# One step of a hybrid recurrent, convolution and MLP layer on one core: two tasks for the bonus and the values of the preparation, and landing times and dependent steps in the scheduling model

## The chip, the core and the metric

The kernel runs on one core of a Trainium2 chip. The metric is device microseconds of one execution, the median of several. The engines are TensorE (PE, matrix products and transposes), VectorE (DVE), ScalarE (ACT), GpSimd (POOL), and SyncE (SP), on whose queue all DMAs of this kernel are issued, one after the other. Tiles lie in SBUF on 128 partitions; PE writes to eight banks of PSUM, which DVE and ACT read.

## The reference

A layer with width D = 1024 for a context of 128 tokens and a latent sequence of 1024, 1152 together:

```
shift_a, scale_a, gate_a, shift_f, scale_f, gate_f = jnp.split(mod[:, None, :], 6, axis=-1)
h = _rmsnorm(x, norm1_g) * (1 + scale_a) + shift_a
z = h @ w_in
...
s_f, y_f = _wkv7_scan(s_f0.astype(f32), rh, heads(dec_f), k_fh, vh, kk, heads(a_f), reverse=False)
s_b, y_b = _wkv7_scan(s_b0.astype(f32), rh, heads(dec_b), k_bh, vh, kk, heads(a_b), reverse=True)
...
bonus = jnp.sum(rh * (k_fh + k_bh) * r_k, axis=-1, keepdims=True) * vh
g = jax.nn.sigmoid(gl) @ w_g2
o_rwkv = (yn + bonus.reshape(b, l, RWKV_WIDTH)) * g
...
mix = jnp.concatenate([o_rwkv.astype(x.dtype), o_conv.astype(x.dtype)], axis=-1) @ w_out
x = (x + gate_a * mix).astype(x.dtype)
h = _rmsnorm(x, norm2_g) * (1 + scale_f) + shift_f
f = jnp.square(jax.nn.relu(h @ w_ff1)) @ w_ff2
x = (x + gate_f * f).astype(x.dtype)
```

`mod` is `silu(c) @ w_mod + b_mod`, 6 x 1024 columns, once for the latent and once for the context vector. The change touches how `bonus` and the part `ln_b * g` that is added to it are made ready.

## The kernel before, in words

Channels lie on partitions, and the 1152 tokens are three groups of 384. Stages follow each other:

- **Startup:** loads and transposes x, makes the first 16 of 48 blocks (128 columns each) of `mod`, which the first norm needs, and `hT`, the normed input in two parts (a rounded one and its rest, so that three products with a split weight make one in full precision).
- **Preparation** (line 1154): for each of 27 column blocks of `w_in`, three groups of 24 matmuls of `hT` with the split weight `w` (`proj_task`), whose results `take_task` turns into `r_g`, `k_g`, `v_g` (three buffers each) and others. `gate_task`, `front_task` (one for each direction) and `kk_task` make the scan's operands from them and store these in DRAM. `value_task` (line 1098) goes over 4 pairs of heads and 3 groups: it adds the two directions' keys `kd_g` into the one buffer `bt_g`, multiplies by r and `r_k`, turns the values v and stores them (8 DMAs to `v_d`), sums over the head with a matmul against `ones_blk`, multiplies by v, makes the gate's product, and stores two arrays of 192 KB in `fin_d`, one from `gl_g`, one from `bt_g`. `mod_task` (line 1132) makes the other 32 blocks of `mod`: each is a DMA of 512 KB into the one buffer `wm`, 16 matmuls, a copy `R` and two small matmuls with `sel`; after the last a matrix of gates is stored in `gate_d`. `warm_task` issues filler matmuls of `ident16`.
- **Chain stage:** a new pool of buffers takes the memory of the preparation's tiles, so that its first loads (`bk`, `qr`) and POOL's fill of `Z` wait for all of that to be done with, the last stores among it. It makes the chunked scan of both directions, 36 steps of loads.
- **x1 stage** (output projection and second norm), **FFN** (first and second product), and a **tail** in which the last output tiles are summed from banks (`facc<-bank,facc`), multiplied by the gate (`late9`), added to x (`late1` and up), normed by ACT (`sf`) and scaled by DVE into the result (`facc<-facc,sf,late11`).

The order in which each engine works is fixed when the program is written, by a scheduler, `class Order` (line 28). Tasks are generators that emit operations, each with its priority. The scheduler keeps for each engine the time at which it is free, and for each tile who read and wrote it until when. `start` (line 82) says when an operation could begin: the latest end of those it depends on, plus a price `HOP` for the way from one engine to another; dependences on the same engine are left out. `run` (line 250) always issues the operation that can begin first, among those within 20 ns the one of the first task. Durations come from formulas at the helpers (`act` line 335, `tt` line 362, `stt` line 377, `dma` line 449). In this model a DMA holds its queue for bytes/350 ns (at least 480) and has landed 1900 ns later. An engine of the chip works strictly in the order so written.

## Time and profile before

| | us |
|---|---|
| median of 3 runs | 1871.28 |
| lowest and highest run | 1868.84, 1874.59 |
| the profiled execution, its own time | 1867.13 |
| its span in the trace | 1865.3 |
| PE busy in the span | 1725.0 (92%) |
| DVE busy | 1170.3 (63%) |
| ACT busy | 572.9 (31%) |

The span is the time from the first to the last instruction that the profiler recorded; the execution's own time is 1.8 us longer. In the page, the chain that ended last is followed back from the last instruction to what released each one, so it tells whose time adds up to the span. A window's busy time against its length tells whether an engine had holes there, and the list of waits says what ended these holes. A row of the timeline holds neighbouring instructions of one form; several rows may overlap, since an engine starts one while the last is still in its pipeline.

### The profile page before, as it was taken

To read this page: it belongs to the slowest core of one execution; us is meant where nothing else is said; L and a number is where in the kernel's file an instruction comes from. 1 tells how busy PE (TensorE), PEld (TensorE's weight loads), DVE (VectorE), ACT (ScalarE), POOL (GpSimd) and SP (SyncE) were. 2 spreads that over 40 slices of the span, in tenths; PEclk is the share of its full clock that TensorE was granted. 3 is DMA by queue.
4 is the path that set the end of the run, shared out by engine and by line. 5 is a ranking of instruction groups with operands and counts; after the bars stand their busy time and mean duration, and the time that the engine had idled before them with its cause. 6 is when DMAs were issued, how large, how long until landed. Compare 5 with 4: busy or idle time off the path is not lost.

```text
span 1865.3 us, 47366 instructions
## 1 busy us (share of the span) xinstructions
PE 1725.0 (92%) x20250; PEld 1535.8 (82%) x20250; DVE 1170.3 (63%) x2481; ACT 572.9 (31%) x1384; POOL 36.0 (2%) x167
## 2 busy tenths in 40 slices
PE   5899999999877878888989999999999999999996
PEld 3788888988767777777767899999999999999995
DVE  3557676777668877777655534555555555555557
ACT  5444344544244444444334421111100010000112
POOL 6000000000000000000000000000000000000000
PEclk9999999999999999999999999999999999999998
DMA  8436666665544443334144311111111111101142
GB/s 297 112 103 161 167 168 162 157 181 137 135 139 134 143 115 101 101 108 126 58 146 131 102 57 46 46 46 46 46 46 46 45 35 46 38 24 42 46 151 97
DMA packets 291449, 190.35 MB, mean 102 GB/s; under 512 B 109171, under 2 KB 274214, under 8 KB 291238
## 3 DMA queue, kind: packets, MB, share of 16 engines
q1 hardware_dynamic: 291238, 187.32, 34.5%
q8 instruction: 159, 2.61, 0.6%
q14 instruction: 52, 0.43, 0.1%
HBM read 137.44 MB, written 49.82 MB: 100 GB/s over the span
## 4 chain that ended last, share of the span: by engine, by line
PE 72%; DVE 8%; DMA 7%; issue 4%; ACT 4%; SPq 3%; DVEq 0%; ACTq 0%; POOL 0%; POOLq 0%
PE bank L440 72%; SPq L451 3%; DMA wm<-in_w_mod_dram 3%; DVE facc L362 1%; PE bank L443 1%; DMA fg<-fin_d 1%; DVE facc L377 1%; DVE x L362 1%; DVE y L362 1%; ACT mx L339 0%; ACT late L339 0%; DMA raw<-o_d 0%; ACT h L400 0%; DVE mx L362 0%; DMA late<-x_d 0%
## 5 line engine op out<-in xcount | busy, mean ns | idle before, releaser
L440 PE MATMUL bank<-hT,w 128*128 128x384 f32 (+1 forms) x2232 | 448.6, 354 | 0.0
L440 PEld LDWEIGHTS bank<-hT,w 128*128 128x128 f32 x2232 | 395.7, 191 | 26.8 <-issue 10.3
L440 PE MATMUL bank<-h,w 128*128 128x384 f32 x2304 | 409.9, 339 | 0.0
L440 PEld LDWEIGHTS bank<-h,w 128*128 128x128 f32 x2304 | 407.3, 188 | 1.2
L440 PE MATMUL bank<-w2f,f1f 128*128 128x512 f32 x1674 | 385.2, 389 | 0.0
L440 PEld LDWEIGHTS bank<-w2f,f1f 128*128 128x128 f32 x1674 | 314.0, 188 | 64.7
L362 DVE TENSOR_TENSOR facc<-bank,facc 128x512 f32<-128x512 f32 x252 | 173.9, 690 | 134.3 <-PE bank L440 133.1
L339 ACT ACTIVATE rl<-bank 128x384 f32<-128x384 f32 x96 | 47.2, 492 | 340.4 <-PE bank L440 340.4
L362 DVE TENSOR_TENSOR rl<-rl 128x384 f32<-128x384 f32 x96 | 53.4, 557 | 154.9 <-ACT rl L339 154.8
L440 PE MATMUL bank<-qr,bk 64*64 64x128 f32 x1152 | 118.6, 285 | 7.2 <-DMA bk<-kb_d 3.5
L384 ACT ACTIVATE cur<-bank 128x256 f16<-128x256 f32 (+1 forms) x286 | 98.2, 383 | 69.3 <-PE bank L440 56.1
L440 PE MATMUL bank<-cur,at 64*64 64x64 f16 x1728 | 87.0, 196 | 11.3 <-issue 6.5
L440 PEld LDWEIGHTS <-cur 64*64 64x64 f16 x2016 | 76.5, 108 | 24.3 <-issue 19.1
L440 PEld LDWEIGHTS <-at 64*64 64x64 f16 x2016 | 77.6, 108 | 19.9 <-issue 15.2
L440 PE MATMUL bank<-P,cur 64*64 64x64 f16 x1728 | 77.3, 198 | 17.4 <-issue 10.5
L362 DVE TENSOR_TENSOR P<-bank,lmask 128x256 f16<-128x256 f32 x180 | 74.8, 419 | 26.4 <-PE bank L440 22.2
L440 PEld LDWEIGHTS bank<-qr,bk 64*64 64x64 f32 x1152 | 77.6, 137 | 8.3 <-issue 7.9
L362 DVE TENSOR_TENSOR w<-raw,w 128x256 fp32r<-128x256 f32 (+3 forms) x149 | 77.1, 553 | 9.5 <-ACT w L339 7.8
L384 ACT ACTIVATE w2f<-raw 128x1024 fp32r<-128x1024 f32 x11 | 11.7, 1061 | 185.0 <-PE bank L440 184.7
L440 PE MATMUL bank<-G,bk 64*64 64x64 f32 x576 | 59.4, 226 | 3.2 <-issue 3.2
L440 PE MATMUL bank<-qr,Z 64*64 64x64 f32 x576 | 57.2, 223 | 3.4 <-issue 3.4
L440 PE MATMUL bank<-cur,P 64*64 64x64 f16 x1152 | 57.6, 198 | 2.8 <-issue 2.7
(251 smaller groups left out, 2479.9 us busy)
## 6 DMA issues: line engine op xcount, KB each, us to landing
raw<-in_w_ff_dram SPq DMA_DIRECT2D x43, 512.0 KB
wm<-in_w_mod_dram SPq DMA_DIRECT2D x32, 512.0 KB
raw<-in_w_in_dram SPq DMA_DIRECT2D x27, 512.0 KB
rf<-in_w_ff_dram SPq DMA_DIRECT2D x21, 512.0 KB
qr_d<-qr_g SPq DMA_DIRECT2D x24, 384.0 KB
kb_d<-kb_g SPq DMA_DIRECT2D x24, 384.0 KB
kt_d<-kt_g SPq DMA_DIRECT2D x192, 48.0 KB
bk<-kb_d SPq DMA_DIRECT2D x72, 128.0 KB
```

The source lines that it names most:

```text
L339: lambda e: se.activation(out=out, in_=in_, func=func, **kw),
L362: lambda e: ENG[e].tensor_tensor(out=out, in0=a, in1=b, op=op))
L377: lambda e: ve.scalar_tensor_tensor(out=out, in0=a, scalar=s, in1=b, op0=op0, op1=op1))
L384: lambda e: se.activation(out=out, in_=in_, func=AF.Copy) if e == "act"
L440: pe_op(out, lhsT, rhs, lambda e: te.matmul(out, lhsT=lhsT, rhs=rhs, start=start, stop=stop, **kw))
L443: pe_op(out, in_, identity, lambda e: te.transpose(out=out, in_=in_, identity=identity), 1)
L451: od.emit([("dma", max(480.0, n / 350.0))], [out], [in_], lambda e: sy.dma_start(out=out, in_=in_), 1900.0)
```

## The change

There are two parts. In the scheduler's model, `start` also counts a dependence on the same engine, on what wrote the operand, with 115 ns on DVE, 150 on ACT and 100 on POOL; an activation that also accumulates costs 150 ns more; and a DMA lands 1900 ns + bytes/200 after its time on the queue, which for the 512 KB of `wm` makes 6.0 us from the issue where it was 3.4. In the preparation, `value_task` is cut in two. `bonus_task` makes the product in `bt_g` and its sum over the head in a bank that it holds, one at a time; `value_task` turns and stores the values, makes the gate's product, multiplies the held bank by v into v's own buffer, frees the bank, and stores the second array from there, so that `v_g` is free only with that store's issue. The number of operations that these tasks make is unchanged.

```diff
--- before.py
+++ after.py
@@ -38,6 +38,9 @@
     HOP = {("pe", "dve"): 205.0, ("pe", "act"): 205.0, ("dve", "pe"): 145.0, ("act", "pe"): 175.0,
            ("act", "dve"): 150.0, ("dve", "act"): 130.0, ("act", "pool"): 170.0, ("pool", "dve"): 80.0,
            ("dve", "pool"): 150.0, ("pool", "act"): 110.0, ("pool", "pe"): 150.0}
+
+
+    SAME = {"dve": 115.0, "act": 150.0, "pool": 100.0}
     SLACK = 20.0
     GLUE = -1.0
     LOAD = 1290.0
@@ -88,8 +91,12 @@
         for wr, bs in ((False, bi), (True, bo)):
             for nm, p0, p1, f0, f1 in bs:
                 for q0, q1, g0, g1, te_, en, w in self.log.get(nm, ()):
-                    if (wr or w or nm in self.banks) and p0 < q1 and q0 < p1 and f0 < g1 and g0 < f1 and en != eng:
-                        t = max(t, te_ + self.HOP.get((en, eng), 70.0))
+                    if p0 < q1 and q0 < p1 and f0 < g1 and g0 < f1:
+                        if en != eng:
+                            if wr or w or nm in self.banks:
+                                t = max(t, te_ + self.HOP.get((en, eng), 70.0))
+                        elif w and en in self.SAME:
+                            t = max(t, te_ + self.SAME[en])
         return t
 
     def emit(self, opts, outs, ins, fn, tail=0.0, pe=None, table=None):
@@ -334,7 +341,7 @@
 
     def act(out, in_, func=AF.Copy, **kw):
         x = aps(kw.get("scale"), kw.get("bias"))
-        d = (52 if in_psum(in_) else 94) + 47 * len(x) + size(in_) / 1.2
+        d = (52 if in_psum(in_) else 94) + 47 * len(x) + size(in_) / 1.2 + (150 if "accum_out" in kw else 0)
         od.emit([("act", d)], [out] + aps(kw.get("accum_out")), [in_] + x,
                 lambda e: se.activation(out=out, in_=in_, func=func, **kw),
                 table=TABLES.get(func))
@@ -448,7 +455,8 @@
 
     def dma(out, in_):
         n = size(out) * 4 * out.ap[0][1]
-        od.emit([("dma", max(480.0, n / 350.0))], [out], [in_], lambda e: sy.dma_start(out=out, in_=in_), 1900.0)
+        od.emit([("dma", max(480.0, n / 350.0))], [out], [in_], lambda e: sy.dma_start(out=out, in_=in_),
+                1900.0 + n / 200.0)
 
     def split(src, hi, lo, eng="dve"):
 
@@ -1095,37 +1103,48 @@
                     turned(kt_d[j, d, :, cs].rearrange("p c a k -> p (c a) k"), t)
                     flag(kt_g.append, t)
 
+        bonus = []
+
+        def bonus_task():
+
+            t = bt_g[0]
+            for j in range(4):
+                for g in range(NN):
+                    q = 3 * j + g
+                    yield lambda: (j, g, 0) in kd_done and (j, g, 1) in kd_done
+                    tt(t, kd_g[0], kd_g[1], ALU.add)
+                    mark(done, ("kd", q))
+                    yield lambda: ("r", j, g) in got
+                    stt(t, r_g[q % 3], par("rk", j), t, ALU.mult, ALU.mult)
+                    use(q, "r")
+                    yield lambda: ("v", j, g) in got and len(bonus) == 0
+                    ps = ps_get([128, NW])
+                    bank = hold(ps)
+                    mm(ps, ones_blk, t)
+                    flag(bonus.append, (ps, bank))
+
         def value_task():
             for j in range(4):
                 for g in range(NN):
                     gs = slice(g * NW, (g + 1) * NW)
                     q = 3 * j + g
-                    yield lambda: (j, g, 0) in kd_done and (j, g, 1) in kd_done
-
-                    t = bt_g[0]
-                    tt(t, kd_g[0], kd_g[1], ALU.add)
-                    mark(done, ("kd", q))
-                    yield lambda: ("r", j, g) in got
-                    stt(t, r_g[q % 3], par("rk", j), t, ALU.mult, ALU.mult)
-                    use(q, "r")
 
 
                     yield lambda: ("v", j, g) in got
                     v, vt = v_g[q % 3], vt_g[0]
                     blocks_t(vt.rearrange("p c h k -> p (c h k)"), v)
                     turned(v_d[j, :, 6 * g:6 * g + 6, :], vt)
-                    ps = ps_get([128, NW])
-                    mm(ps, ones_blk, t)
-                    tt(t, ps, v, ALU.mult)
-                    use(q, "v")
-                    yield lambda: ("sg", g) in got
+                    yield lambda: ("sg", g) in got and len(bonus) > 0
+                    pb, bank = bonus.pop(0)
                     ps = ps_get([128, NW])
                     mm(ps, lw_g[:, 128 * j:128 * j + 128], sg_s[:, gs])
+                    tt(v, pb, v, ALU.mult)
+                    free(bank)
                     mul(gl_g[0], ps, par("lnw", j))
-                    stt(t, t, par("lnb", j), ps, ALU.add, ALU.mult)
+                    stt(v, v, par("lnb", j), ps, ALU.add, ALU.mult)
                     dma(fin_d[j, 0, :, gs], gl_g[0])
-                    dma(fin_d[j, 1, :, gs], t)
-
+                    dma(fin_d[j, 1, :, gs], v)
+                    use(q, "v")
 
         PACE1 = 8000.0
 
@@ -1152,7 +1171,7 @@
 
         numbered = list(enumerate(blocks))
         od.run([(0, part(sp, lambda: False)), (1, gate_task(), 4), (1, front_task(0), 0), (1, front_task(1), 0), (0, kk_task()),
-                (2, value_task(), 2), (3, proj_task(numbered), 2), (1, take_task(81), 0), (2, mod_task(), 2),
+                (2, bonus_task(), 2), (2, value_task(), 2), (3, proj_task(numbered), 2), (1, take_task(81), 0), (2, mod_task(), 2),
                 (9, warm_task(lambda: nproj[0] >= 2))])
 
         fs.close()
```

As the model sets the order of all stages, the order changes in many places. Three follow. The names are tiles with their buffer's number, and the line numbers of the changed kernel are 7 higher.

PE in the middle of the preparation, a stretch with blocks of `mod` (`wm`, 16 matmuls, of which the order shows eight in a row) among projection matmuls (`hT`); before:

```order
L440 MATMUL bank0_94<-wm_800,sc_105 32x128 x8
L440 MATMUL bank2_96<-hT_73,w2_1_69 128x384 x3
L440 MATMUL bank1_95<-sel_107,R1_801 128x2
L440 MATMUL bank2_96<-hT_73,w2_1_69 128x384 x2
L440 MATMUL bank0_94<-hT_73,w2_0_68 128x384 x14
L440 MATMUL bank5_99<-wm_800,sc_105 32x128 x8
L440 MATMUL bank0_94<-hT_73,w2_0_68 128x384 x3
L440 MATMUL bank1_95<-kk_j0_831,ones_blk_120 128x384
L440 MATMUL bank2_96<-sel_107,R1_801 128x2
L440 MATMUL bank0_94<-hT_73,w2_0_68 128x384 x7
L440 MATMUL bank2_96<-hT_73,w2_0_68 128x384 x7
L440 MATMUL bank5_99<-wm_800,sc_105 32x128 x8
```

and now:

```order
L447 MATMUL bank0_94<-wm_780,sc_105 32x128 x8
L447 MATMUL bank1_95<-hT_73,w2_1_69 128x384 x3
L447 MATMUL bank5_99<-sel_107,R1_781 128x2
L447 MATMUL bank1_95<-hT_73,w2_1_69 128x384 x4
L447 MATMUL bank0_94<-hT_73,w2_0_68 128x384 x19
L447 MATMUL bank5_99<-kk_j0_811,ones_blk_120 128x384
L447 MATMUL bank0_94<-hT_73,w2_0_68 128x384 x5
L447 MATMUL bank4_98<-wm_780,sc_105 32x128 x8
```

Between the uses of `wm` stood 19 and 17 matmuls of `hT`, and now 31 stand between two.

SP's queue at the end of the preparation, from a group's `fin_d` on (`v_d` are the values, `o_d` the convolution's result, `bk0` the chain stage's first load); before:

```order
L451 DMA fin_d_81<-gl_g0_833 128x384
L451 DMA fin_d_81<-bt_g0_832 128x384
L451 DMA gate_d_88<-R1_801 32x128
L451 DMA v_d_85<-vt_g0_829 32x6x32 x8
L451 DMA fin_d_81<-gl_g0_833 128x384
L451 DMA fin_d_81<-bt_g0_832 128x384
L451 DMA bk0_4736<-kb_d_83 128x256
```

and now:

```order
L458 DMA wm_780<-in_w_mod_dram 128x8x128
L458 DMA fin_d_81<-gl_g0_813 128x384
L458 DMA fin_d_81<-v_g1_807 128x384
L458 DMA v_d_85<-vt_g0_809 32x6x32 x4
L458 DMA o_d_86<-oc0_831 128x384
L458 DMA v_d_85<-vt_g0_809 32x6x32 x4
L458 DMA wm_780<-in_w_mod_dram 128x8x128
L458 DMA fin_d_81<-gl_g0_813 128x384
L458 DMA fin_d_81<-v_g2_808 128x384
L458 DMA gate_d_88<-R1_781 32x128
L458 DMA bk0_4715<-kb_d_83 128x256
```

The loads of the last two blocks of `mod` (`wm`) now stand among the last stores, and `gate_d` behind the last `fin_d`.

DVE in the tail, one output tile after the other; before:

```order
L362 TENSOR_TENSOR facc_17188<-bank2_96,facc_17188 128x512
L377 SCALAR_TENSOR_TENSOR facc_17188<-facc_17188,sf_17187,late11_21766 128x1024
L362 TENSOR_TENSOR facc_17188<-bank0_94,facc_17188 128x512
L362 TENSOR_TENSOR facc_17188<-facc_17188,late9_21764 128x1024
L362 TENSOR_TENSOR facc_17188<-facc_17188,late2_21757 128x1024
L362 TENSOR_TENSOR facc_17188<-bank5_99,facc_17188 128x512
L377 SCALAR_TENSOR_TENSOR facc_17188<-facc_17188,sf_17187,late11_21766 128x1024
```

and now:

```order
L369 TENSOR_TENSOR facc_17167<-bank7_101,facc_17167 128x512
L369 TENSOR_TENSOR facc_17167<-facc_17167,late1_21735 128x1024
L369 TENSOR_TENSOR facc_17167<-bank6_100,facc_17167 128x512
L369 TENSOR_TENSOR facc_17167<-facc_17167,late9_21743 128x1024
L384 SCALAR_TENSOR_TENSOR facc_17167<-facc_17167,sf_17166,late11_21745 128x1024
L369 TENSOR_TENSOR facc_17167<-bank3_97,facc_17167 128x512
L369 TENSOR_TENSOR facc_17167<-facc_17167,late2_21736 128x1024
L369 TENSOR_TENSOR facc_17167<-bank1_95,facc_17167 128x512
L369 TENSOR_TENSOR facc_17167<-facc_17167,late9_21743 128x1024
L384 SCALAR_TENSOR_TENSOR facc_17167<-facc_17167,sf_17166,late11_21745 128x1024
```

Before, the scaling (`sf`) comes behind one bank sum of the next tile; now it comes behind that and the product of the next tile with `late9`.

## Rows read from the trace of the kernel before

**Rows 1.** The page, part 4: the chain of work that ended last, its share of the span by engine.
```profile
PE 72%; DVE 8%; DMA 7%; issue 4%; ACT 4%; SPq 3%; DVEq 0%; ACTq 0%; POOL 0%; POOLq 0%
```

**Rows 2.** The windows by stage, core 0: start and end, us, busy us (x instructions) of PE, PE's weight loads, DVE, ACT and POOL, then granted clock of PE, DMA share and GB/s. In order: startup, preparation up to the end of the last projection matmul, the end of the preparation, chain stage, x1 stage, FFN, tail.
```profile
0.00:66.00 66.00, 41.79 (x392) 27.94 (x392) 32.83 (x82) 40.91 (x77) 32.22 (x135) 0.94 0.84 264
66.00:505.20 439.20, 423.68 (x2669) 381.76 (x2670) 303.98 (x665) 187.01 (x414) 2.61 (x24) 0.98 0.56 147
505.20:522.30 17.10, 7.63 (x15) 3.63 (x13) 5.03 (x10) 5.94 (x10) 0.24 (x2) 0.78 0.46 128
522.30:945.00 422.70, 355.51 (x12697) 313.38 (x12698) 324.11 (x959) 187.02 (x578) 0.91 (x6) 0.98 0.39 112
945.00:1057.00 112.00, 103.85 (x488) 84.89 (x488) 64.36 (x101) 46.76 (x119) 0.00 (x0) 0.98 0.44 143
1057.00:1801.00 744.00, 744.00 (x3781) 684.41 (x3780) 393.51 (x614) 90.08 (x149) 0.00 (x0) 1.00 0.14 43
1801.00:1865.30 64.30, 48.54 (x215) 39.83 (x213) 46.48 (x51) 15.20 (x39) 0.00 (x0) 0.90 0.44 172
```

**Rows 3.** The timeline of PE at the start of the preparation: start us, busy us, engine, line, operation, out<-in and shapes, count, and in brackets the idle time before it and what ended it.
```profile
66.07 0.59 PE L440 MATMUL bank<-sel,R 128*128 128x2 f32 x2 [3.35 <-ACT R L384]
```

**Rows 4.** The chain of work in the preparation, two of its pieces, loads of `wm`: start us, us from issue to landing.
```profile
230.11 3.81 DMA wm<-in_w_mod_dram
...
430.02 5.86 DMA wm<-in_w_mod_dram
```

**Rows 5.** The waits of PE from 66 to 505.2: engine, tile and line, what it waited for, us in total, times, longest us.
```profile
PE bank L440 <- DMA wm<-in_w_mod_dram: 14.3, 16, 2.8
PE bank L440 <- ACT R L384: 3.4, 1, 3.4
PE bank L440 <- ACT kk_j L339: 0.8, 1, 0.8
```

**Rows 6.** The timeline of PE in the preparation: the first row of a block of `w_mod` after a wait, twice, and a long run of projection matmuls in between.
```profile
180.05 0.88 PE L440 MATMUL bank<-wm,sc 128*32 128x128 f32 x16 [2.42 <-DMA wm<-in_w_mod_dram]
...
441.80 19.49 PE L440 MATMUL bank<-hT,w 128*128 128x384 f32 x111
...
484.71 1.08 PE L440 MATMUL bank<-wm,sc 128*32 128x128 f32 x16 [2.81 <-DMA wm<-in_w_mod_dram]
```

**Rows 7.** Windows in the preparation, columns as in rows 2 (the granted clock is the number after the five engines).
```profile
180.00:190.00 10.00, 9.95 (x71) 9.32 (x75) 5.79 (x13) 4.31 (x9) 0.11 (x1) 0.83 0.72 179
370.00:390.00 20.00, 17.73 (x116) 16.26 (x115) 10.38 (x23) 8.55 (x21) 0.22 (x2) 0.91 0.67 175
480.00:500.00 20.00, 17.18 (x96) 16.45 (x96) 14.59 (x31) 3.04 (x8) 0.00 (x0) 0.83 0.49 140
```

**Rows 8.** The timeline of DVE at the start of the chain stage: two operations of which the second reads what the first wrote, and a row of two that don't depend on each other.
```profile
524.35 0.69 DVE L362 TENSOR_TENSOR G<-bank,wmask 128x512 f32<-128x512 f32 x1 [7.59 <-PE bank L440]
525.07 0.29 DVE L362 TENSOR_TENSOR at<-G,eye 128x128 f16<-128x128 f32 x1
...
533.28 0.76 DVE L362 TENSOR_TENSOR P<-bank,lmask 128x256 f16<-128x256 f32 x2 [0.51 <-ACT cur L384]
```

**Rows 9.** The chain of work at the end of the preparation: start us, us, what.
```profile
509.06 2.09 DMA fin_d<-bt_g
...
511.24 0.57 DVE bt_g L362
...
517.35 1.95 DMA fin_d<-bt_g
```

**Rows 10.** The timeline of SP's queue there: start us, us on the queue, engine, line, what, count.
```profile
512.97 3.70 SPq L451 DMA_DIRECT2D v_d<-vt_g  x8
...
519.42 0.32 SPq L451 DMA_DIRECT2D bk<-kb_d  x1
```

**Rows 11.** The waits of PE in the chain stage, 522.3 to 945.
```profile
PE bank L440 <- issue: 42.1, 55, 1.8
PE bank L440 <- DVE P L362: 5.5, 14, 1.6
...
PE bank L440 <- DVE Al L377: 2.3, 2, 1.3
```

**Rows 12.** The waits of PE in the x1 stage, 945 to 1057.
```profile
PE bank L443 <- DVE mx L371: 4.4, 7, 1.3
```

**Rows 13.** The timeline of DVE in the tail: one output tile in the middle, and the last two bank reads.
```profile
1812.12 1.28 DVE L377 SCALAR_TENSOR_TENSOR facc<-facc,sf,late 128x1024 f32<-128x1024 f32 x1 [1.18 <-ACT sf L339]
...
1814.04 2.48 DVE L362 TENSOR_TENSOR facc<-facc,late 128x1024 f32<-128x1024 f32 x2
...
1818.30 1.28 DVE L377 SCALAR_TENSOR_TENSOR facc<-facc,sf,late 128x1024 f32<-128x1024 f32 x1 [1.18 <-ACT sf L339]
...
1856.81 0.68 DVE L362 TENSOR_TENSOR facc<-bank,facc 128x512 f32<-128x512 f32 x1
1857.53 1.42 DVE L362 TENSOR_TENSOR facc<-facc,late 128x512 f32<-128x512 f32 x2
```

**Rows 14.** The timeline of PE in the tail: the last of a bank's matmuls in the middle, and the last of all.
```profile
1816.06 0.84 PE L440 MATMUL bank<-w,f1f 128*128 128x512 f32 x3
...
1848.70 0.84 PE L440 MATMUL bank<-w,f1f 128*128 128x512 f32 x3
```

**Rows 15.** The page, part 6: the DMA issues of one form, count and size of each.
```profile
bk<-kb_d SPq DMA_DIRECT2D x72, 128.0 KB
```

## The prediction

> **What bounds the kernel now.** I read the chain of work first, then the windows by stage, then the waits and the timeline of each stage in which the engine named there stood still. The chain is TensorE (PE) for 72% of the span, and transfers are 7% of it [rows 1]. So the time is PE's work plus the stretches in which PE stands still, and a stage is worth looking at only where PE has holes. By stage PE's busy time and holes are [rows 2]: startup 41.8 of 66.0 us; preparation 423.7 of 439.2; its end, a gap of 17.1 us in which the last projection is done and the chain stage has no data, 7.6 busy; chain stage 355.5 of 422.7; x1 stage 103.9 of 112.0; FFN 744.0 of 744.0; tail 48.5 of 64.3.
>
> The profiled execution took 1867.13 us for a span of 1865.3; the median of the three runs shown is 1871.28, 4.15 above it. I sum against the profiled execution and add 4.15 at the end. A measurement of this kernel can tell about 0.3% (5.6 us) from no change.
>
> **The change, part by part.** No engine gets or loses more than a handful of operations: twelve multiplications change their operands, one bank is held longer, some 20 filler matmuls go. What changes is the order.
>
> *Startup.* PE's long hole at its end is 3.35 us for an `R` copy [rows 3], which stands on ACT behind three pairs of an h and an hT copy, each of which waits for VectorE (DVE). In the new order it stands behind one pair less. A third of the hole is 1.1; bounds are the whole hole (−3.4) and, if the second weight load comes later behind the loads of `wm`, +1. I take −1.
>
> *Preparation: when the 32 blocks of `w_mod` land.* All share one buffer: a block's 16 matmuls wait for its load, and the next load for them. The model had a landing 3.4 us after the issue (1.5 of queue, 1.9 of tail), the rows have 3.81 to 5.86 [rows 4]. Since the scheduler believed the shorter figure, it put block matmuls too early, and PE, which is in order, stood there with the projection matmuls queued behind: 14.3 us in 16 waits, at most 2.8 [rows 5]. Between such uses stood 17 to 20 projection matmuls in the worst places, and one takes 0.176 us (19.49/111, [rows 6]): 3.0 to 3.5 us of cover for loads of 3.8 and more. The changed model has 6.0 us (1.5+1.9+2.6). Of the 31 distances between two blocks 9 were at most 20 matmuls; in the new order it is one of the first 29, and most are 26 to 160, 4.6 us and more. I take −12 of the 14.3. The bounds are −14.3, and −5 if SP issues the loads late, since it works in order and a load also stands behind stores whose data come late.
> The same figure bears the Trainium skill's rule on the price of a transfer ("DMA: Bandwidth & Descriptors", section "Anatomy of one DMA — SWDGE (gpsimd) path": about 2.0 us fixed plus the bytes over 436 GB/s, for another issue path than this one). For 512 KB that is an estimate of 3.2 us, close to the old model, by which the old distances would hardly stall and this term would be about −3. The loads in the rows are 0.6 to 2.7 us longer, so here the trace decides.
>
> *The clock behind the waits.* The granted clock fell in three places: its mean was 0.83 in the 10 us from 180, 0.91 in the 20 from 370 and 0.83 in the 20 from 480 [rows 7], mixtures of the full 2.4 and of 1.2 GHz, and 1.7, 1.8 and 3.4 us are lost there, together 6.9. The holes of 2.42 us up to 180.05 and of 2.81 up to 484.71 [rows 6] lie right before or in them. If the holes go, these go: −5, bounds −6.9 and 0.
>
> *The last two blocks.* In the new order their matmuls stand behind the last projection matmul: 2 x 0.64 to 0.88 us [rows 6] leave the stretch, −1.5 with their copies' small holes, and go to the end of the preparation, below.
>
> *New waits.* `value_task` now waits for a bank that `bonus_task` fills, and the bonus matmul waits for DVE's product. PE has the projections to put there. Same-engine steps get 115 to 150 ns more in the model, and rows show a dependent operation only 0.03 us behind its predecessor's end (524.35+0.69 to 525.07, [rows 8]), so the new model is wrong there by some 0.1 us, in the direction that leaves slack. I put +3.5 for stalls that the order creates elsewhere (0 to +8; the waits of PE in this stretch other than for `wm` sum to 4.2 now, [rows 5]). Preparation: −12−5−1.5+3.5 = **−15**, from −24 to 0.
>
> *The end of the preparation.* Before, the last group's bonus was late because `bt_g` was released only when its store had landed, 2.09 us after its issue: the last sum is at 511.24, the last store is issued at 517.35 and lands 1.95 later [rows 9], and the first load of the chain stage is issued at 519.42 [rows 10], 14.2 us after the last projection matmul (505.2, the border in [rows 2]). POOL's fill of `Z` waits for the same store. Now `bt_g` comes free at its matmul, and the last bonus is done under the projections; that chain is gone. But something else is late: the load of the last `w_mod` block stands on SP behind the store of a group's results, eight stores of values and one of `o_d`, and it waits for the block before, whose 16 matmuls stand behind the last projection. By the rows: eleven issues of 3.70/8 = 0.46 us [rows 10], the first when the values are ready, about 0.9 before that matmul's end (an estimate), so the issue is at +4.1, the landing at +8.2 (4.1, nearer to the short end of [rows 4]), 16 matmuls at half the clock to +9.4, copy, selection, the gate's transpose and copy (five steps of about 0.5) to +12, the store of `gate_d`, its landing of 2 us [rows 9] at +14.1. First load at +14.1 against +14.2: **0**, bounds −2 and +3.
>
> *Chain stage.* Nothing is edited, but the order of DVE changes: pairs in which an operation reads what the one just before it wrote fall from 58 to 23. Two independent ones of 0.42 us took 0.76 together, so the second started 0.08 before the first's end; the dependent one starts 0.03 after [rows 8]: 0.11 x 35 = 3.9 us of DVE's time. PE's waits for DVE in the stage are 5.5 (`P`) and 2.3 us (`Al`); its largest is 42.1 of unnamed "issue" [rows 11], which this doesn't touch. I take −3. Since a new order of 12,700 matmuls may fall either way, the bounds are −8 (all of these waits) and +10.
> The Trainium skill's "VectorE: DVE Perf Modes", section "The DRAIN you can't avoid", has the next operation held until the pipe is empty, semaphore or not, so that reordering earns nothing. The 0.34 us between the starts of two operations of 0.42 us disagrees. This is rival B.
>
> *x1 stage.* Such pairs 74 to 46; PE waits 4.4 us for `mx` of DVE [rows 12]. 28 x 0.11 = 3.1 at most, mostly off the path: −1 (−3 to +2).
>
> *FFN.* Pairs 210 to 140, but PE is busy 744.0 of 744.0 at clock 1.00 and DVE for 393.5 [rows 2]: 0. If that cover fails, 70 x 0.11 = 7.7 us.
>
> *Tail.* This I can count. Before, DVE's period for one output tile is 6.18 us (1812.12 to 1818.30), of which it idles 1.18 for ACT's `sf` (the last scaling stands right behind the tile's own sum and has to wait for square, sum and root); PE's is 5.44, two banks of (1848.70−1816.06)/12 = 2.72 [rows 13, 14]. So DVE is the bound: PE ends at 1849.54, and the last read of a bank is at 1856.81. In the new order the next tile's bank sum (0.68) and first product (2.48/2 = 1.24) stand between, 1.92 us, more than the 1.78 that ACT now takes from the end of the tile's own sum (1814.04+2.48 = 1816.52) to its scaling at 1818.30. DVE's work per tile is then 6.18−1.18 = 5.0 us, under PE's 5.44, so PE sets the pace and DVE has no backlog: last bank read at about 1849.6+0.3, then sum, products and sum of the last tile 0.70+0.72+1.25+0.72+0.72 to 1854.0, where before it was 1858.95 (1857.53+1.42). **−5** (−5.5 to −3.5: one tile may still wait).
>
> Sum: −1−15+0−3−1+0−5 = **−25**. 1867.13−25 = 1842.1; with 4.15 for the median, 1846.
>
> **The rivals.** A: the waits of the preparation *move*. The blocks come no later than PE asks because SP is in order, behind stores of 0.4 us each, and what is not lost in the preparation comes at its end, when the last blocks hold the first loads. For it: in the new order the last two blocks do stand behind the last projection. Against: the early distances did grow. Preparation −3 instead of −15, end +4: 1846+12+4 = 1862.
> B: the DVE reordering earns nothing (chain and x1 stage 0): 1846+4 = 1850.
> C: the chain stage gains more, since PE's 42.1 us of "issue" are really short waits for DVE and ACT that the trace names nothing for, and a third of them goes: 1846−12 = 1834.
> D, slower: the chain stage is 36 steps (72 loads of `bk`, two directions [rows 15]), 11.7 us each, and DVE is busy 324 of its 423 us. If a too careful model puts an operation on the chain's way ahead of the next link in each step, this costs its length: one `G` product of 0.69 us [rows 8] is 36 x 0.69 = 25, 1849+25 = 1874, no change; a `G` and a `P` product (0.69+0.42) are 40, 1889. It ends slower above 0.77 us a step ((25+5.6−3)/36). Against: the model's new term is small and DVE has 99 us free.
>
> **How the numbers follow.** Forecast 1846: 0.48. A 0.17, B 0.12, C 0.10, D with one product 0.08, with two 0.05. The range 1834 to 1862 takes in C's and A's times and the bounds of the unknown terms nearest to the forecast (chain stage −8 to +10). Faster by over 0.3% (below 1865.7): forecast, A, B, C, 0.87, less 0.02 for an A that gets worse: 0.85. Within 0.3%: 0.08+0.02 = 0.10. Slower (above 1876.9): 0.05.
>
> **What would show it.** PE's waits for `wm` fall from 14.3 to about 2, and no window of the preparation shows a clock under 0.95; first `bk` load 14 us behind the last projection matmul, with `gate_d` and no longer `fin_d` ahead of it; the chain stage within 10 us of 423; in the tail the wait for `sf` on DVE falls from 8.8 us to under 2, and the last bank read follows PE's end by about 5 us. Wrong would be: waits for `wm` that stay above 8 us, a first load later than 17 us behind the last projection, or a chain stage beyond 433 us.

## The result, and the profile after

| | before | after |
|---|---|---|
| median, us | 1871.72 (4 runs) | 1819.38 (4 runs) |
| lowest and highest | 1868.84, 1874.59 | 1815.72, 1826.61 |
| the profiled execution, its own time | 1867.13 | 1815.72 |
| its span | 1865.3 | 1814.0 |

The ratio is 0.9725, interval 0.969 to 0.9761: 2.75% faster, against 1846 and 1834 to 1862 forecast. The gain is twice the forecast one and lies outside the range.

To compare stages I cut both traces at the same events: end of the last projection matmul, then the starts of the first matmul of the chain stage (`qr,bk`), of its last (`G,bk`), of the first of the FFN (`h,w`) and of the last of all, and the end. The windows after (columns as in [rows 2]), without the startup:

```profile
60.70:481.10 420.40, 415.90 (x2648) 373.55 (x2648) 310.26 (x683) 175.91 (x399) 3.61 (x24) 1.00 0.59 155
481.10:497.60 16.50, 7.25 (x48) 4.19 (x48) 2.77 (x8) 6.40 (x13) 0.24 (x2) 0.69 0.48 137
497.60:899.10 401.50, 343.11 (x12625) 306.09 (x12625) 313.85 (x942) 181.59 (x574) 0.91 (x6) 0.98 0.40 115
899.10:1003.20 104.10, 102.58 (x520) 83.49 (x515) 63.68 (x105) 49.41 (x124) 0.00 (x0) 1.00 0.46 148
1003.20:1803.30 800.10, 800.10 (x4040) 731.88 (x4039) 428.91 (x647) 113.33 (x203) 0.00 (x0) 1.00 0.17 54
1803.30:1814.00 10.70, 0.43 (x2) 0.01 (x1) 5.71 (x8) 3.54 (x10) 0.00 (x0) 0.65 0.26 108
```

and before at these events, where [rows 2] has other borders:

```profile
61.50:505.20 443.70, 424.89 (x2688) 382.46 (x2689) 306.42 (x670) 190.17 (x421) 2.61 (x24) 0.98 0.56 146
...
522.30:930.70 408.40, 343.20 (x12621) 304.55 (x12621) 317.01 (x945) 183.04 (x570) 0.91 (x6) 0.98 0.40 113
930.70:1048.80 118.10, 108.12 (x516) 86.06 (x517) 67.66 (x110) 47.58 (x119) 0.00 (x0) 0.97 0.40 131
...
1849.20:1865.30 16.10, 0.34 (x2) 0.00 (x0) 10.95 (x13) 3.59 (x11) 0.00 (x0) 0.61 0.24 98
```

| us | before | after | difference | forecast |
|---|---|---|---|---|
| startup and preparation | 505.2 | 481.1 | −24.1 | −16 |
| end of the preparation | 17.1 | 16.5 | −0.6 | 0 |
| chain stage | 408.4 | 401.5 | −6.9 | −3 |
| x1 stage | 118.1 | 104.1 | −14.0 | −1 |
| FFN | 800.4 | 800.1 | −0.3 | 0 |
| behind the last matmul | 16.1 | 10.7 | −5.4 | −5 |
| span | 1865.3 | 1814.0 | −51.3 | −25 |

The x1 stage alone holds half of what the forecast lacks. Not only PE's idle time fell there (10.0 to 1.5 us) but its busy time too (108.12 to 102.58). The granted clock was 0.97 and is 1.00, which is 3.5 us of 118.1. Of the other 2 us about half is work that left the stage: from one cut to the next the traces have 260 matmuls of `hT` by `w` of 0.227 us before, and 255 after.

PE's waits in the preparation after, where [rows 5] had 14.3 us for `wm` and 3.4 for `R`:

```profile
PE bank L447 <- ACT kk_j L346: 3.6, 4, 1.9
PE bank L447 <- DMA wm<-in_w_mod_dram: 1.6, 2, 0.9
```

PE's waits in the x1 stage, before and then after:

```profile
PE bank L443 <- DVE mx L371: 4.2, 6, 1.3
PE bank L443 <- ACT h L400: 3.7, 1, 3.7
PE bank L440 <- DVE y L362: 2.0, 1, 2.0
```

```profile
PE bank L450 <- DVE mx L378: 0.9, 2, 0.5
PE bank L447 <- ACT f L346: 0.6, 1, 0.6
```

Of 9.9 us 1.5 are left. Where the two large ones came from, ACT's timeline before shows (the row behind the dots is a copy of a loaded block of `o_d`, on which the `h` rows follow):

```profile
958.74 1.06 ACT L339 ACTIVATE mx<-x 128x1024 f32<-128x1024 f32 x1 [2.72 <-issue]
959.70 0.18 ACT L339 ACTIVATION_READ_ACCUMULATOR mx<-x 128x1 f32 x1
959.92 0.29 ACT L339 ACTIVATE ss<-ss,eps 128x1 f32<-128x1 f32 x1
960.25 0.20 ACT L339 ACTIVATE ss<-ss 128x1 f32<-128x1 f32 x1
...
969.62 0.31 ACT L384 ACTIVATE hT<-raw 128x128 fp32r<-128x128 f32 x1 [4.78 <-DMA raw<-o_d]
969.84 5.69 ACT L400 ACTIVATE h<-bank,modc,s 128x128 f32<-128x128 f32 x16
```

```profile
960.48 0.75 DVE L371 TENSOR_SCALAR mx<-x,ss 128x1024 f32<-128x1024 f32 x1 [0.17 <-ACT ss L339]
```

```profile
971.38 0.66 PE L443 MATMUL bank<-ident,mx 128*128 128x128 f32 x4 [3.65 <-ACT h L400]
```

First, the statistics: from the start of the square (958.74) to the start of the scaling into `mx` on DVE (960.48) are 1.74 us. By the formulas of the old model this is 947 (square) + 142 + 95 (the two small activations) + 150 (to DVE) = 1.33 us; by the new one, with 150 for the accumulator and 150 behind each, 1.78. So PE's transposes of `mx` were planned 0.4 us too early by this, and PE waited for `mx` six times. Second, the copy of a loaded block waited 4.78 us for its DMA on ACT, which is in order, with the 16 `h` rows behind it, for which PE stood 3.65 us. Both are the same fault as with `wm`: the model believed a thing ready that was not. But for this load of 64 KB the new price is no truer to speak of: 2.4 us from the issue in the old model, 2.7 in the new one, and 4.6 in the trace (issued at 964.93, landed at 969.54).

The tail on DVE after, where [rows 13] had 1.18 us idle ahead of each scaling and the last bank read 7.3 us behind PE's end:

```profile
1800.20 1.28 DVE L384 SCALAR_TENSOR_TENSOR facc<-facc,sf,late 128x1024 f32<-128x1024 f32 x1
...
1803.77 0.69 DVE L369 TENSOR_TENSOR facc<-bank,facc 128x512 f32<-128x512 f32 x1
1804.38 0.68 DVE L369 TENSOR_TENSOR facc<-facc,late 128x512 f32<-128x512 f32 x1
...
1809.15 1.28 DVE L384 SCALAR_TENSOR_TENSOR facc<-facc,sf,late 128x1024 f32<-128x1024 f32 x1 [0.60 <-ACT sf L346]
```

Of DVE's waits for `sf` in the tail, 8.8 us before by the prediction, this is left:

```profile
DVE facc L384 <- ACT sf L346: 1.8, 2, 1.2
```

The last bank read starts at 1803.77, just at PE's end, 1803.73 (last row below):

```profile
1802.89 0.84 PE L447 MATMUL bank<-w,f1f 128*128 128x512 f32 x3
```

The end of the preparation after, SP's queue and PE:

```profile
483.29 1.91 SPq L458 DMA_DIRECT2D v_d<-vt_g  x4
485.30 0.40 SPq L458 DMA_DIRECT2D wm<-in_w_mod_dram  x1
...
486.41 0.38 SPq L458 DMA_DIRECT2D fin_d<-v_g  x1
493.01 0.33 SPq L458 DMA_DIRECT2D gate_d<-R  x1
494.53 0.33 SPq L458 DMA_DIRECT2D bk<-kb_d  x1
```

```profile
489.64 1.08 PE L447 MATMUL bank<-wm,sc 128*32 128x128 f32 x16 [5.75 <-DMA wm<-in_w_mod_dram]
491.17 0.59 PE L447 MATMUL bank<-sel,R 128*128 128x2 f32 x2 [0.45 <-ACT R L391]
```

The load of the last block of `w_mod` stands behind the stores, PE waits 5.75 us for it, `gate_d` follows at 493.01 and the first `bk` load at 494.53, 13.4 us behind the last projection matmul.

### The profile page after: what moved, and what is told of

It is laid out like the page before. It is cut to its first block, busy times and chain, and to the rows that moved or that the text cites. A ratio compares the mean times of both kernels' runs of the same rounds, so it can differ in the third digit from the quotient of the medians.

```text
span 1814.0 us, 47292 instructions
## 1 busy us (share of the span) xinstructions
PE 1709.2 (94%) x20229; PEld 1527.7 (84%) x20229; DVE 1156.1 (64%) x2470; ACT 568.8 (31%) x1395; POOL 37.7 (2%) x167
## 4 chain that ended last, share of the span: by engine, by line
PE 80%; DVE 6%; issue 4%; DMA 4%; SPq 3%; ACT 2%; DVEq 0%; POOL 0%; ACTq 0%; POOLq 0%
PE bank L447 79%; SPq L458 3%; DMA wm<-in_w_mod_dram 2%; PE bank L450 1%; DMA zs<-in_state_rwkv_fwd_dram 0%; ACT cur L391 0%; DVE w L369 0%; DMA raw<-o_d 0%; DMA kt_d<-kt_g 0%; DVE facc L369 0%; ACT kk_j L346 0%; DVE kt_g L454 0%; DVE kb_g L369 0%; DMA xt<-in_x_sample_dram 0%; ACT h L407 0%
## 5 line engine op out<-in xcount | busy, mean ns | idle before, releaser
L447 PE MATMUL bank<-hT,w 128*128 128x384 f32 (+1 forms) x2232 | 439.9, 349 | 0.0
L447 PEld LDWEIGHTS bank<-hT,w 128*128 128x128 f32 x2232 | 388.1, 188 | 25.6 <-issue 9.8
L447 PEld LDWEIGHTS bank<-h,w 128*128 128x128 f32 x2304 | 407.3, 188 | 1.2
L447 PE MATMUL bank<-qr,bk 64*64 64x128 f32 x1152 | 115.9, 286 | 5.1 <-issue 2.9
L447 PEld LDWEIGHTS <-cur 64*64 64x64 f16 x2016 | 75.3, 108 | 21.1 <-issue 15.9
L447 PE MATMUL bank<-cur,at 64*64 64x64 f16 x1728 | 83.0, 196 | 7.9 <-issue 5.4
L369 DVE TENSOR_TENSOR w<-raw,w 128x256 fp32r<-128x256 f32 (+3 forms) x149 | 78.0, 553 | 17.5 <-ACT w L346 13.3
L391 ACT ACTIVATE w2f<-raw 128x1024 fp32r<-128x1024 f32 x10 | 10.6, 1061 | 184.7 <-PE bank L447 184.7
```

The source lines that it names most:

```text
L369: lambda e: ENG[e].tensor_tensor(out=out, in0=a, in1=b, op=op))
L391: lambda e: se.activation(out=out, in_=in_, func=AF.Copy) if e == "act"
L447: pe_op(out, lhsT, rhs, lambda e: te.matmul(out, lhsT=lhsT, rhs=rhs, start=start, stop=stop, **kw))
```

## The experiments

All stage lengths below are cut at the same events; "wm" is PE's wait for `wm` from 60 us up to the last projection matmul (in e2 and n1 one wait of 5.1 and one of 5.0 us of it end at 63 us, ahead of the preparation). The chain stage before is cut 0.2 us earlier here than above, at its last matmul's start. Each ratio is against runs of the kernel before on the same chip; the stages come from one profile each, and the chips differ: one for e1 to e4, others for n1 to n3 and m0, for e5, s1, a0 and k0, and for e6, e7, a1 and m1.

| run | ratio (95%) | last projection | gap | chain | x1 | tail | wm |
|---|---|---|---|---|---|---|---|
| before | | 505.2 | 17.1 | 408.2 | 118.3 | 16.1 | 14.3 |
| after | 0.9725 (0.969 to 0.9761) | 481.1 | 16.5 | 401.5 | 104.1 | 10.7 | 1.6 |
| e1_landing | 0.9901 (0.9883 to 0.9919) | 474.3 | 42.4 | 407.3 | 109.4 | 16.5 | 0.3 |
| e2_steps | 0.9866 (0.9846 to 0.9886) | 490.9 | 22.7 | 402.8 | 110.1 | 10.7 | 17.5 |
| e3_two_tasks | 0.9924 (0.9902 to 0.9946) | 501.1 | 10.8 | 403.4 | 116.9 | 16.2 | 9.3 |
| n1_no_landing | 0.9839 (0.9812 to 0.9865) | 494.4 | 13.8 | 397.8 | 108.1 | 10.7 | 15.9 |
| n2_no_steps | 0.9928 (0.9906 to 0.995) | 478.0 | 41.9 | 395.9 | 106.2 | 16.2 | 2.2 |
| n3_no_split | 0.9788 (0.9768 to 0.9807) | 471.7 | 32.5 | 397.2 | 103.5 | 10.6 | 0 |
| e4_steps_late | 0.9936 (0.9916 to 0.9957) | 503.7 | 18.6 | 409.0 | 111.6 | 10.6 | 13.4 |
| e5_landing_late | 0.9987 (0.9972 to 1.0001) | 503.0 | 18.0 | 411.2 | 116.5 | 16.3 | 13.1 |
| e6_act_steps_late | 0.9943 (0.9923 to 0.9964) | 507.1 | 17.1 | 403.3 | 110.9 | 10.8 | 13.9 |
| e7_dve_steps_late | 0.995 (0.9929 to 0.997) | 505.9 | 16.8 | 401.0 | 115.3 | 12.3 | 14.3 |
| s1_other_order | 0.9975 (0.9958 to 0.9991) | 502.0 | 19.1 | 408.6 | 115.9 | 16.1 | 14.6 |
| a0_after_again | 0.9717 (0.969 to 0.9743) | 481.2 | 17.2 | 398.1 | 104.0 | 10.7 | 0.9 |
| k0_one_task_blocks_first | 0.9738 (0.9712 to 0.9765) | 483.6 | 18.8 | 403.0 | 104.8 | 10.6 | 2.0 |
| m0_blocks_first | 0.9708 (0.9689 to 0.9728) | 477.6 | 13.2 | 397.5 | 104.8 | 10.6 | 0 |
| a1_after_beside | 0.97 (0.9655 to 0.9745) | 479.2 | 16.3 | 394.9 | 103.8 | 10.7 | 0.2 |
| m1_blocks_first_beside | 0.9675 (0.9633 to 0.9717) | 477.4 | 13.4 | 390.0 | 104.8 | 10.6 | 0 |

**One part alone** (e1 to e3). The edits are the three parts of the diff above, each put into the kernel before by itself.

e1: 

> The kernel before with one line changed: a DMA lands 1900 ns + bytes/200 after its queue time in the model. Theory (each part of the change acts where its model was wrong): the waits of PE for wm fall from 14.3 to under 4 us and the last projection matmul ends near 486 instead of 505.2; x1 stage (last matmul of the chain to the first of the FFN) stays at 118 +- 4 us, tail behind the last matmul at 15.8; about 1852. Rival (any new order falls another way, whatever the model says): the preparation gains under 8 us, or the x1 stage moves by more than 8.

e2: 

> The kernel before with the dependent steps alone (same-engine prices and 150 ns for an accumulating activation). Theory: x1 stage 118.2 to about 105, tail behind the last matmul 15.8 to 10.5, chain stage 408 to about 403, preparation within 4 us of 505.2 with the waits for wm still above 10; about 1848. Rival (any new order): the x1 stage moves by less than 5 us or the preparation by more than 10.

e3: 

> The kernel before with bonus and values as two tasks, the model untouched. Theory: the waits for wm stay (over 10 us), the gap between the last projection matmul and the chain stage's first matmul falls from 17.1 to 11 to 15 us, x1 stage and tail unchanged; 1866 to 1873. Rival (the two tasks carry the preparation's gain): the last projection matmul ends 10 us or more earlier, 1860 or less.

e1 behaves as the theory says in the preparation, and far beyond: the last projection ends 31 us earlier, the wait for `wm` is gone, and the gap behind it grows from 17 to 42 us, which the theory did not have. Its chain of work there (start us, us, what):

```profile
488.56 3.90 DMA wm<-in_w_mod_dram
492.51 1.12 PE bank L440 x16
493.65 3.88 DMA wm<-in_w_mod_dram
497.57 1.13 PE bank L440 x16
...
```

Five blocks of `w_mod` now stand behind the last projection, one load and 16 matmuls after the other, 5.05 us each, since all share one buffer. This is the mechanism of my rival A, at full size, and landing times alone do it. The x1 stage moved by 9 us where the theory had 4 at most; that is the rival's sign (more than 8), and e5 takes it up. e2: the tail as expected, the x1 stage at 110 where I had 105; but the preparation gained 14 us with the wait for `wm` at 17.5, so the theory missed there, and the rival's sign (more than 10) came in; the last section has the reason. e3: the gap fell to 10.8 and the waits for `wm` to 9.3, both under what I gave, and the total to 0.9924, below it too; 5 us of it stand in the chain stage. In its order the last block stands 359 projection matmuls ahead of the end, and what is left is the last group's stores.

**One part left out** (n1 to n3).

n1: 

> The changed kernel with the old landing time (1900 ns): steps and two tasks alone. Theory (the landing time takes the preparation's waits away and by itself also pushes the last blocks of w_mod behind the projections): waits for wm above 10 us again, last projection matmul 490 to 496 instead of 481.1, but the last block is 365 projection matmuls early, so the gap to the chain stage is 9 to 13 us instead of 16.5; tail 10.6; about 1826. Rival (the landing time does nothing of the gain once the steps are right): 1819 or less.

n2: 

> The changed kernel without the dependent steps: landing time and two tasks. Theory (steps carry the tail and part of the x1 stage; without them the blocks of w_mod are late again, six of them stand behind the last projection matmul): tail 16, x1 stage 108 to 114, gap to the chain stage 40 to 55; 1848 to 1862. Rival (the two tasks carry the end of the preparation, not the steps): gap under 20, 1830.

n3: 

> The changed kernel with bonus and values in one task as before: landing and steps. Theory (the split only shortens the end of the preparation): last projection matmul 478 to 486, gap 20 to 27 instead of 16.5, x1 stage 102 to 108, tail 10.6; 1822 to 1832. Rival (the split is needed for most of the gain): above 1840.

Totals were written against 1871.7, and on this chip the kernel before took 1859.53; measured were 1826.63 (n1), 1845.66 (n2) and 1817.73 (n3). By stages n1 and n2 came as the theory has it, but for a gap of n1 0.8 us longer (13.8) and an x1 stage of n2 2 us shorter; n1's total is 0.9839 where 1826 of 1871.7 is 0.976, so the landing time is worth more beside the other two than I gave. n3's tail and x1 stage came too; its preparation is shorter (471.7) and its gap longer (32.5) than I gave. Seen at the chain stage's first matmul (last projection plus gap) the parts add up: from 522.3 landing takes 5.6 us, steps 8.7 and the two tasks 10.4, 24.7 in sum, and all three together take 24.7 (497.6). That is a coincidence: left out of the three, landing is worth 10.6 us there (n1, 508.2), steps 22.3 (n2, 519.9) and the two tasks 6.6 (n3, 504.2), 39.5 in sum. What the landing time gains before the last projection (31) it gives back in the gap (25); beside it the steps shorten the gap by 25 us (n2's 41.9 to 16.5) and the two tasks by 16 (n3's 32.5), while the steps alone lengthen it (e2, 22.7). In totals, 1.0, 1.3 and 0.8% alone make 3.1, against 2.75 to 3.0 for all, which tells as little.

**From the x1 stage on only** (e4 to e7). Everything up to there keeps the order of before; the model is switched at the call that plans the x1 stage (the last hunk of e4's edit, without its other lines).

```diff
+        od.SAME = {"dve": 115.0, "act": 150.0, "pool": 100.0}
         od.run([(0, part(ot, lambda: False), 0), (0, part(o3t, lambda: False), 0), (1, x1_task(0)), (1, x1_task(1))] +
```

e4: 

> The kernel before with the dependent steps counted only from the x1 stage on (x1, FFN, tail); everything up to there is in the order of before. Theory (the statistics' steps on ACT were believed too short, so that PE's transposes stood too early): nothing moves up to 930 us, x1 stage 118.2 to 104 to 110, tail 15.8 to 10.5; about 1855. Rival (the x1 stage's gain came from what it took over from the chain stage, or by luck): x1 stage 115 to 121, only the tail gains, 1866.

e5 (the landing time in place of the steps): 

> The kernel before with the new landing time only from the x1 stage on; everything up to there is in the order of before. Theory (ACT's copy of a loaded o_d block stood in the queue ahead of the h rows for which PE's transposes waited 3.65 us; a truer landing puts it behind): no wait of PE for ACT h over 1.5 us, x1 stage 118.3 to 108 to 114, tail unchanged at 16; about 0.996 of before. Rival (e1's shorter x1 stage was carried over from the chain stage): x1 stage 116 to 121, ratio 0.999 to 1.001.

e6 (of the steps ACT's alone): 

> The kernel before with ACT's steps alone (150 ns after its own writer, 150 ns for an accumulating activation) from the x1 stage on. Theory (the row of small activations between a tile's sum and its scaling was believed too short): tail 10.6, waits for mx under 2.5 us, x1 stage 111 to 115; 0.993 to 0.996. Rival (DVE's steps carry it): tail 15 to 16, waits for mx above 3.5.

e7 (DVE's alone): 

> The kernel before with DVE's steps alone (115 ns after its own writer) from the x1 stage on. Theory (ACT's steps carry it): the scaling still stands ahead of the next product in the tail, 14 to 16 us, waits for mx 3 to 5 us, x1 stage 115 to 119; 0.998 to 1.000. Rival: tail 10.6, x1 stage 112 or less.

PE's waits in the x1 stage of e4 and of e5:

```profile
PE bank L445 <- DVE y L367: 1.7, 1, 1.7
PE bank L448 <- ACT h L405: 1.6, 1, 1.6
PE bank L448 <- DVE mx L376: 1.4, 4, 0.6
```

```profile
PE bank L444 <- DVE mx L372: 6.4, 7, 1.5
PE bank L441 <- DVE y L363: 1.9, 1, 1.9
```

Against 4.2 (`mx`), 3.7 (`h`) and 2.0 (`y`) before: the steps take `mx` to 1.4 and halve `h`; the landing time takes `h` away, as the theory has it, but `mx` rises to 6.4, so that the stage gains 2 us (116.5, as the rival has it) and the total nothing that can be told. So a hole removed by one price is given back at the place where the model is still wrong. That both together from the x1 stage on would make the 14 us is not shown, since no run has just that. Nor are steps needed for most of it: with landing and two tasks planned throughout, and no steps, n2 has 106.2 us and a clock of 1.00 in the stage, and e1, with landing alone, 109.4. Part of that is work that stands ahead of the stage there (248 matmuls of `hT` by `w` in it for 260, about 2.7 us); why the landing time gains the rest from the start on (n2 12 us, e1 9) and only 2 from the x1 stage on stays open. e4's total is 0.9936, where I had 1855 of 1871.7, 0.991, and its x1 stage 2 us longer than I gave. e6 carries the tail and as much of the x1 stage as e4, as expected; e7's tail (12.3), its wait for `mx` (2.2) and its total lie below what I gave, so DVE's steps do part of it too.

**Another order without a truer model** (s1: slack of 40 ns for 20).

```diff
-    SLACK = 20.0
+    SLACK = 40.0
```

> The kernel before with the scheduler's slack at 40 ns instead of 20: another order with no truer model in it. Theory (orders as such don't gain): total within 0.7% of before, x1 stage 113 to 122, tail 15.5 to 16.5, waits for wm above 8 us; single stages may move 5 us either way. Rival (before was an unlucky order and any other gains 1% or more): ratio 0.99 or less.

Every stage and wait stays within about 3 us of before, total −0.25%, as the theory has it. That a new order as such brings 1% or more is refuted for this one other order.

**The blocks of `w_mod` first** (m0, k0, a0, a1, m1).

```diff
-                (2, bonus_task(), 2), (2, value_task(), 2), (3, proj_task(numbered), 2), (1, take_task(81), 0), (2, mod_task(), 2),
+                (2, bonus_task(), 2), (2, value_task(), 2), (3, proj_task(numbered), 2), (1, take_task(81), 0), (1, mod_task(), 2),
```

m0: 

> The changed kernel with the priority of the task that makes the blocks of w_mod at 1 instead of 2: the last block then stands 504 projection matmuls ahead of the end instead of behind it, and 22 or more stand between any two. Theory (of the 16.5 us at the end of the preparation some 7 are the last blocks): gap 8 to 11, waits for wm under 4 us, the rest as in the changed kernel; about 1812. Rival (the gap is held by the last stores of values anyway): gap 15 to 17, 1819.

k0: 

> Landing and steps with bonus and values in one task, and the blocks of w_mod at priority 1. Theory (what the one task costs at the end is mostly the blocks that it leaves behind the projections): last projection matmul 470 to 477, gap 15 to 20 (the store of bt_g before the last bonus stays), ratio 0.967 to 0.973, within 4 us of m0_blocks_first. Rival (the split is needed): gap over 25, ratio 0.976 or more.

a0: 

> The changed kernel once more, beside the others of this call. Both theories: ratio to before 0.969 to 0.976; stages as in its first profile (481.1, gap 16.5, chain 401.5, x1 104.1, tail 10.7) within 3 us.

a1: 

> The changed kernel, on the chip of the next run. Both theories: ratio 0.969 to 0.976, gap 16 to 17.5.

m1: 

> The changed kernel with the blocks of w_mod at priority 1, on the chip of the run before. Theory (the last blocks hold the first loads, and the rest is as before): 5 to 10 us under the changed kernel, of them 3 at the gap. Rival (the two are the same and the first comparison was one of two chips): within 3 us.

With the blocks first the gap is 13.2 and 13.4 against 16.3 to 17.2: 3 us of it were the last blocks, not the 7 that I expected (m0's 8 to 11 us; its rival had 15 to 17), because eight stores of values and the last `fin_d` then end last:

```profile
481.40 3.74 SPq L458 DMA_DIRECT2D v_d<-vt_g  x8
485.23 0.39 SPq L458 DMA_DIRECT2D fin_d<-gl_g  x1
485.72 0.38 SPq L458 DMA_DIRECT2D fin_d<-v_g  x1
487.80 0.32 SPq L458 DMA_DIRECT2D bk<-kb_d  x1
```

The chain stage's first matmul comes at 490.8 in both, against 495.5 to 498.4 in the three profiles of the changed kernel. On one chip (a1, m1) the medians are 1807.18 and 1803.74, with runs that overlap: about 0.2%, between my 5 to 10 us and the rival's 3, which these runs don't settle. k0's gap is 14 us shorter than n3's, but its last projection comes 12 us later, against my 470 to 477: in the preparation PE is busy 5.6 us longer (415.5 for 409.9), with three blocks that n3 has behind the last projection, and idle 4.7 us longer. Its gap of 18.8 refutes the rival's 25; its ratio of 0.9738 lies between theory and rival, and the interval (0.9712 to 0.9765) holds both 0.973 and 0.976. On the same chip the changed kernel has 1813.89 us and k0 1817.79, 0.2%, so what the split is worth with the blocks first is small and not settled.

## Why the prediction came out too small

*Right, with size:* the waits for `wm`: 14.3 to 1.6, −12.7 where I took −12; new waits +2.8 (`kk_j` 0.8 to 3.6) where I took +3.5; the end of the preparation step by step: last load issued 4.2 us behind the last projection, its matmuls 8.5, `gate_d` 11.9 and the first load 13.4, where I had 4.1, 8.2, 12 and 14.1 (though e3 shows that I gave the two tasks too little: alone they take 10.4 us off the way to the chain stage, 6.3 of it in the gap); the FFN; the tail, −5.4 where I had −5, with DVE in step with PE.

*The step that failed* is the x1 stage, "28 x 0.11 = 3.1 at most, mostly off the path: −1 (−3 to +2)", and the reading of the model behind it, "the new model is wrong there by some 0.1 us". I set the model's 115 ns against the gap between two busy times in the trace. But the model adds it to its own duration, which is 69 + 512 x 1.04 = 601 ns for the product of [rows 8]: 716 ns from start to start, and the row has 0.72. So the new price of a step was true there, not careful, as it was for ACT (1.78 for 1.74 us above), and what it is worth is not DVE's time but PE's holes, where PE's operation had been planned too early. I had the holes in front of me (4.4 for `mx` in [rows 12]) and valued them by the wrong engine; the 3.7 for `h`, a landing time, I didn't value at all. Holes of 9.9 us and 3.5 of clock (3% of 118.1) were there to be won; of the 14.0 won 8.5 are idle time, 3.5 the clock and 2 neither, about half of it work that left the stage. e4 and e6, with before's order up to the stage, show that steps do a half (6.7 and 7.4 us, with PE's waits at 4.7 and 5.9). By what the other half came is open: landing from the stage on gains 1.8 (e5), but planned throughout it gains 8.9 alone (e1) and 12.1 beside the two tasks (n2).

*Mis-sized* in the preparation: the clock, "−5, bounds −6.9", which I summed over three places only. The fourth begins right behind the hole for `R`, and 0.82 over 18.49 us are 3.3 us lost:

```profile
61.51:80.00 18.49, 15.14 (x100) 13.97 (x101) 5.88 (x16) 5.02 (x13) 0.15 (x2) 0.82 0.20 58
```

The stage's mean of 0.98 is some 9 us over 443.7, and after it is 1.00. And the hole for `R`, of which I took a third; it is gone in whole (3.4). Together with the rest −24.1 for −16, just at the bound that I had written for the preparation alone, −24 (the bounds of its terms sum to −22.7 and +1.5, not to the −24 and 0 that I wrote).

*The chain stage* gave −6.9 where I had −3, inside the bounds; but kernels with before's order up to there have 401.0 to 411.2 us (before, e4 to e7), and the changed kernel 394.9 to 401.5. On the same chip it is 398.1 against 411.2 (a0, e5) and 394.9 against 403.3 and 401.0 (a1, e6, e7). So it gained, and how much is not settled. PE's wait for DVE's `P`, 5.5 us in [rows 11] and 3.7 to 5.5 in those five, is 1.5 to 1.9 in the three profiles of the changed kernel, so a part likely came from the term that I had named:

```profile
PE bank L447 <- DVE P L369: 1.9, 6, 0.6
```

*The rivals.* B, that the order with DVE's steps earns nothing, is refuted by e7, where DVE's steps alone take the tail from 16.1 to 12.3 us and PE's waits for `mx` from 4.2 to 2.2; its x1 stage of 115.3 is no shorter than that of s1 (115.9) to speak of. The Trainium skill's rule that I put beside it ("VectorE: DVE Perf Modes", section "The DRAIN you can't avoid") has the next operation wait until the pipe is empty, and says too that one that is not held starts earlier. The rows have both, a dependent one 0.03 us behind the end and an independent one 0.08 ahead of it. What I missed is that the gain lies in PE's order knowing this time, not in saving it. A, for which I gave 0.17, is what the landing time does without the steps (e1, n2); the steps prevent most of it, the two tasks the rest (n3, 32.5). C's place, the chain stage's "issue", did not move (42.1 before, 44.7 after), and a third of it is 14 us, not the 12 that I took. D did not show.

My range was too narrow because I bounded the x1 stage by a count of operations and not by all of its holes, of which [rows 2] showed 8.2 us idle and a clock of 0.98. One sign was ill written: the last bank read "about 5 us" behind PE's end does not fit my own sum, which has 0.3; it came at 0.04 us, and the last tile's sum ended 3.9 us behind PE's end where mine has 4.5. The sign of the clock held but for one window (0.91 from 393.5 to 411.0 us, behind a wait of 1.85 us for `kk_j`).

## What to carry to other kernels

A scheduler's price that is too low shows as holes on the engine that is planned in time and executes in order: sum the bound engine's holes by what ended them, add the clock lost behind them, and ask of each whether the model now knows that time. That sum is about the most that a truer model can win there, and the time of the engine that gets the new price is not. A longer landing time can also push a chain of loads with one buffer behind the stage's last work, so look at what stands behind the last matmul of a stage, and put such a chain early by priority. Repair one wrong price and the hole can move to the next one (e5).

## What the runs showed of the chip that I had not expected

The granted clock fell behind single long waits and did not follow their sum. Before, PE has four waits above 2 us in the preparation, 3.35 for `R` [rows 3] and 2.42, 2.27 and 2.81 for `wm`, and the clock's four dips stand behind them ([rows 7] and the window from 61.51 above). In e2 PE waits 17.5 us for `wm` in 16 waits, at most 5.1, more than before, and yet the clock from 63 us on is 1.00:

```profile
63.00:490.90 427.90, 413.88 (x2675) 373.81 (x2676) 304.10 (x672) 178.31 (x405) 3.21 (x22) 1.00 0.57 151
```

```profile
PE bank L445 <- DMA wm<-in_w_mod_dram: 17.5, 16, 5.1
```

The longest of these waits ends where that window begins:

```profile
63.05 1.08 PE L445 MATMUL bank<-wm,sc 128*32 128x128 f32 x16 [5.15 <-DMA wm<-in_w_mod_dram]
```

The 15 others sum to 12.4 us and are at most 1.5 each, and only the first 18 us behind the long one have a lower clock (0.91). So of the 14 us that e2 gained in the preparation some 8 are clock that before had lost behind its long waits, and some 5 idle time (18.8 to 14.0), 3.4 of them the hole for `R`.

And one order of the chain stage took between 401.0 and 411.2 us in five profiles, on at least three chips: its length can't be compared to better than some 5 us from single profiles.
